# A gated MLP on one core: the order of the first products, the evictions and the casts

## The chip, the core and the metric

The kernel runs on one core of a Trainium2 chip. A core has TensorE (PE in the profile, with its weight loads shown apart as PEld), VectorE (DVE), ScalarE (ACT), GpSimd (POOL) and SyncE (SP, which here only issues transfers). They run side by side and meet at semaphores. Matrix products go to PSUM, eight banks of 512 fp32 values on each of 128 partitions; DVE and ACT take them out to SBUF. The metric is the device time of one execution in microseconds; lower is better.

## The reference

```python
def reference(x, w1, w2):            # x: 16 x 256 x 512, w1: 512 x 4096, w2: 2048 x 512, all fp32
    h = x @ w1
    gate, value = np.split(h, 2, axis=-1)
    h = np.maximum(gate, 0) * value
    return (h @ w2).astype(np.float32)
```

The 16 x 256 rows are 4096 tokens. The first layer makes 2048 gate and 2048 value columns for each, their gated product g is the input of the second layer.

## The kernel before

**Tiles and stages.** The tokens go through in four sets of 1024 (`s` from 0 to 3), each in two halves of 512 (`TH`). A set has a first layer of 16 blocks `jb` (128 hidden columns each, gate and value) and a second layer. Both layers are computed with seven products P1 to P7 in place of eight, on sums of the operands: `x_S1` to `x_S4` are sums of quarters of x (`x_sum`, line 451, on DVE), T1 to T4 are sums of quarters of the weights (`w1_one`, line 160, written to `wt` by POOL in set 0), and `g_S1` to `g_S4` are the sums of quarters of g (`g_sum`, line 275, on POOL and DVE) for the second layer. Operands are fp16, sums in PSUM fp32.

**Hybrid blocks.** Class `Block` holds the seven products, each of two 128x512 matmuls through `mm` (line 202). P1 goes to a bank X, ACT copies it to a bank Y (line 209); P2 adds to X, so it must come after that copy; P5 and P3 go to a bank W, P6, P7 and P4 add to Y. ACT and DVE combine the banks into g (lines 216 to 242). `SLOT` and `PERIOD` put the products of neighbouring blocks in a fixed interleaved order.

**Plain blocks.** In set 0 the weight sums are not there at the start, so the first four blocks (`NPLAIN`) are computed in the plain way, class `Plain`: `mm(side, a, q, n)` runs four matmuls (line 259) over the contraction for the gate (side 0, bank X) or the value (side 1, bank W), for quarter `q` of 256 tokens, or for both with `n = 2`. `close(h)` has ACT scale the value out of W (line 264) and DVE make g from it and X (line 265).

**The opening.** SP loads the first 512 tokens of x in fp32 (`xf`) and the first weight chunk (`wl`, gate half and value half), two transfers each, alternating (lines 406 and 407). POOL's queue loads everything else of the weights, and the second 512 tokens as fp16 (`xh`). `turn_pair(xo, b0)` transposes two 128-token blocks of x on PE into two W banks; DVE takes out the even block and ACT the odd one, into `x_A1` (line 377). `cast_w(g_)` casts one half of the first weight chunk to fp16: two of the four contraction quarters by ACT (line 391), two by DVE (line 392). `turn_half` does the transposes of the second 512 tokens, through an X bank (line 384 takes them out). `idle` issues matmuls with no use, to occupy PE while it waits for data.

**Buffers.** X has three PSUM banks, Y three, W two; transposes share the W and X banks with the products. All five engines' orders are written out by hand: each engine executes its instructions in the order in which the program emits them, and waits in front of one hold up those behind it.

**Set 0 beside the opening.** POOL makes the weight sums of blocks 4 to 15 in order, with the loads of w2 between (lines 523 to 539): T1 to T4 of blocks 12 to 15 come last, as four operations of 128x1024. They are followed by the sums of w2's quarters, made by accumulating transfers (`add_w2`, line 163), the fp16 copy of the next x (`cast_x`, line 359), and then `g_S1` and `g_S3` for rows 0 to 3 and `g_S1` for rows 4 and 5. At the end of set 0's first layer DVE makes `g_S1` for rows 6 and 7, then `g_S2`, `g_S4` and the second half of `g_S3` (lines 571 to 575). The second layer (`mm2_stream`, line 286) starts with products that need no sums (X), then P5 needs `g_S1`, P6 needs `g_S2`, P3 `g_S4`, P7 `g_S3`. Most of a set's second layer runs before the next set's first layer begins, the rest inside it.

Of the kernel before, what the change touches and what calls it, by code (L numbers as in the profile page):

```python
# [18 lines left out]
PERIOD = 7  # L19
NWARM = 8  # L20
NFILL = 2
NPLAIN = 4
HIGH, LOW = 512.0, 32.0
GS = 2.0 ** -19
SLOT = {"P1": 0, "P5": 1, "P2": 3, "P6": 4, "P3": 5, "P7": 9, "P4": 13}
# [74 lines left out]
def fast_way(ctx, tc, x2, w1, w2, out2, flag):  # L100
# [54 lines left out]
    def w1_ops(eng, jb, n):  # L155
        for t in TURNS:
            w1_one(eng, jb, n, *t)

    def w1_one(eng, jb, n, m, a, b, o):
        eng.tensor_tensor(W(m, jb, n), W(a, jb, n), W(b, jb, n), op=o)  # L160

    def add_w2(m, v):
        nc.gpsimd.dma_start(out=V[m], in_=V[v], accum_op=ADD)
# [7 lines left out]
    def idle(n):  # L171
        for _ in range(n):
            t = psy.tile([P, TH], F32, name="Y", tag="Y")
            nc.tensor.matmul(t, warm_b[:, :P], warm_b[:, :TH], start=True, stop=True)

    def x_tiles():
        o = {f"A{h}": xpool.tile([P, 4, TH], F16, name=f"x_A{h}") for h in (1, 2)}
        for h in (1, 2):
            for k in (1, 2):
                o[f"A{h}{k}"] = o[f"A{h}"][:, 2 * k - 2:2 * k]  # L180
        for n in ("S1", "S2", "S3", "S4"):
            o[n] = xpool.tile([P, 2, TH], F16, name=f"x_{n}")
        return o
# [88 lines left out]
    def g_sum(eng, go, n, h0, h1):  # L272
        for m, i0, i1, op in SUMS:
            if m == n:
                eng.tensor_tensor(go[n][:, h0:h1], go[i0][:, h0:h1], go[i1][:, h0:h1], op=op)  # L275
# [69 lines left out]
    def advance(stream, n):  # L345
        for _ in range(n):
            if stream is None or next(stream, 0) == 0:
                return
# [5 lines left out]
    def fetch_w2(i):  # L354
        ks, n = slice(i // 2 * NHC, i // 2 * NHC + NHC), i % 2
        nc.gpsimd.dma_start(out=w2_h[n][:, ks], in_=w2_v[:, ks, n * HALF:(n + 1) * HALF])

    def cast_x(s):
        nc.gpsimd.dma_start(out=x16[s], in_=x2[s * SET:(s + 1) * SET, :])

    def g_tiles():
        g = gpool.tile([P, NJ, SET], F16, name="g")
        gs = {n: gpool.tile([P, NHC, TH], F16, name=f"g_{n}") for n in ("S1", "S2", "S3", "S4")}
        return g, g_ops(g, gs)

    g, go = g_tiles()
# [4 lines left out]
    def turn_pair(o, b0):  # L371
        for b in (b0, b0 + 1):
            ps = psw.tile([P, 4, P], F32, name="W", tag="W")
            for e in range(4):
                nc.tensor.transpose(ps[:, e], xf[:, b, e * P:(e + 1) * P], ident[F32])
            copy = nc.scalar.copy if b % 2 else nc.vector.tensor_copy
            copy(out=o["A1"][:, :, b * P:(b + 1) * P], in_=ps)  # L377
# [8 lines left out]
    def turn_by_dma(s, o, h):  # L386
        for k in range(2):
            nc.sync.dma_start_transpose(out=o[f"A{h + 1}{k + 1}"], in_=x16[s][h * TH:(h + 1) * TH, k * 256:k * 256 + 256])

    def cast_w(g_):  # L390
        nc.scalar.copy(out=wr[0][:, :2, g_], in_=wl[:, :2, g_])
        nc.vector.tensor_copy(out=wr[0][:, 2:, g_], in_=wl[:, 2:, g_])
# [3 lines left out]
    def fetch_rows(s, q):  # L396
        rows[s, q] = xpool.tile([P, 2, D], F16, name=f"xn{q % 2}")
        nc.sync.dma_start(out=rows[s, q], in_=x16[s][q * 256:(q + 1) * 256].rearrange("(b p) d -> p b d", p=P))

    def look_x(s, i):  # L400
        b = i // 2
        t = rows[s, b // 2][:, b % 2] if s else (xf, xh)[b // NB][:, b % NB]
        look(t[:, i % 2 * 256:i % 2 * 256 + 256], 4 * NB * s + i, 256)
# [14 lines left out]

    xo = x_tiles()
    plain = [Plain(g, jb) for jb in range(NPLAIN)]  # L420
    idle(NWARM)
    cast_w(0)
    turn_pair(xo, 0)
# [2 lines left out]
    plain[1].open_x()  # L426
    for p in plain[:2]:
        p.mm(0, xo["A1"], 0)
    cast_w(1)
    turn_pair(xo, 2)  # L430
    for p in plain[:2]:
        p.open_w()
        p.mm(1, xo["A1"], 0)
    for p in plain[:2]:
        p.mm(0, xo["A1"], 1)
        p.mm(1, xo["A1"], 1)
        p.close(0)
    for p in plain[2:]:
        p.open_x()
# [9 lines left out]
    def x_sum(o):  # L449
        n, i0, i1, op = sums.pop(0)  # L450
        nc.vector.tensor_tensor(o[n], o[i0], o[i1], op=op)

    for p in plain:
        p.open_x()
        p.open_w()
        if p is plain[0]:
            for q in range(2):
                p.mm(0, xo["A2"], q)
                p.mm(1, xo["A2"], q)
        else:  # L460
            p.mm(0, xo["A2"], 0, 2)
            p.mm(1, xo["A2"], 0, 2)
        x_sum(xo)
        if p is not plain[-1]:
            p.close(1)
        look_x(0, p.jb)
# [47 lines left out]
    for s in range(NS):  # L514
        if s:
            g, go = g_tiles()
        first = NPLAIN if s == 0 else 0
        blocks = {jb: Block(xo, g, jb) for jb in range(first, NJ)}
        plan = {jb * PERIOD + at: (jb, n) for jb in blocks for n, at in SLOT.items()}
        last = NJ * PERIOD  # L520
        stream = mm2_stream(s, go)
        if s == 0:
            w1_ops(nc.gpsimd, 4, 2)
            fetch_w2(0)
            fetch_w2(1)
            w1_ops(nc.gpsimd, 6, 2)
            fetch_w2(2)
            fetch_w2(3)
            w1_ops(nc.gpsimd, 8, 2)
            w1_ops(nc.gpsimd, 10, 2)  # L530
            for to, v in ((V["T1"], V["B11"]), (v_12, w2_h[1]), (V["T4"], V["B21"])):
                nc.sync.dma_start(out=to, in_=v)
            for t in TURNS:
                w1_one(nc.gpsimd, 12, 4, *t)
                if t[0] == "T2":
                    add_w2("T1", "B12")
                    add_w2("T3", "B22")
            add_w2("T2", "T1")
            cast_x(1)
        for at in range(first * PERIOD, last + PERIOD):  # L540
            if at in plan:
                jb, n = plan[at]
                if n == "P1" and s and jb in (4, 8):
                    fetch_rows(s, 1 + jb // 4)
                if n == "P2" and s == 0 and jb in (11, 13, 15):
                    h = jb - 11
                    if h == 4:
                        add_w2("T4", "T2")
                    for m in ("S1", "S3")[:2 - h // 4]:
                        g_sum(nc.gpsimd, go, m, h, h + 2)  # L550
                getattr(blocks[jb], n)()
                ended = jb - (n == "P7") if n == "P7" or (n, jb) == ("P4", NJ - 1) else -1
                if ended in blocks:
                    blocks[ended].finish()
                if n == "P5":
                    for f in LOOKS.get((s, jb), ()):
                        f()
                if ended >= 0 and s:
                    if ended < NHC:
                        g_sum(nc.gpsimd, go, "S3", ended, ended + 1)  # L560
                        if s == 1 and ended in (1, 4):
                            cast_x(2 + ended // 4)
                    elif ended < NJ - BY_DVE:
                        for m in ("S1", "S2", "S4"):
                            g_sum(nc.gpsimd, go, m, ended - NHC, ended - NHC + 1)
            elif at >= last:
                advance(stream, 4)
            else:
                advance(prev, 4)
        if s == 0:  # L570
            g_sum(nc.vector, go, "S1", 6, 8)
            for m in ("S2", "S4"):
                for h in (0, NHC // 2):
                    g_sum(nc.vector, go, m, h, h + NHC // 2)
            g_sum(nc.vector, go, "S3", NHC // 2, NHC)
        else:
            for m in ("S1", "S2", "S4"):
                g_sum(nc.vector, go, m, NHC - BY_DVE, NHC)
        done = 20
        if s + 1 < NS:  # L580
            xo = x_tiles()
            for h in range(2):
                turn_by_dma(s + 1, xo, h)
            for q in range(2):
                fetch_rows(s + 1, q)
            advance(stream, 100)
            sums = list(SUMS)
            for _ in SUMS:
                x_sum(xo)
            if s == 0:  # L590
                w1_ops(nc.vector, 0, 2)
                w1_ops(nc.vector, 2, 2)
            advance(stream, MM2 - TAIL - 100 - done)
        else:
            advance(stream, MM2)
        prev = stream
# [29 lines left out]
```

## Time and profile before

| | |
|---|---|
| median of 5 runs | 311.81 us (311.71 to 312.69) |
| the profiled execution, its own time | 311.87 us |
| its span, first to last instruction | 310.1 us |
| TensorE's mean granted clock | 0.999 |
| DMA: bytes, mean rate | 30.74 MB, 99 GB/s |

By stage (a table of the busy time of each engine, in us):

| stage, us | PE | DVE | ACT | POOL |
|---|---|---|---|---|
| 0 to 10 | 7.22 | 2.10 | 3.19 | 6.76 |
| 10 to 26 | 15.23 | 9.59 | 7.85 | 11.77 |
| 26 to 63 | 37.00 | 31.75 | 24.89 | 34.17 |
| 63 to 73 | 9.37 | 9.36 | 6.72 | 3.27 |
| 73 to 302 | 229.00 | 163.04 | 145.50 | 92.03 |
| 302 to 310.1 | 3.54 | 1.27 | 0.77 | 0.00 |

In the rows of the profile, "engine line op out<-in" names an instruction by the source line that emits it and by its tiles; X, Y and W are the PSUM banks above. A bracket `[1.1 <-DVE ...]` after a row is the idle time of the engine just before it and what ended it. A chain of waits lists, in order of time, the work on which the end of a stretch depended.

### The profile page before, as it was taken

What the parts mean: (1) busy time and instruction counts of PE and PEld (TensorE: products, weight loads), DVE (VectorE), ACT (ScalarE), POOL (GpSimd) and SP (SyncE); (2) the same over time, 40 slices, a digit from 0 to 9 for tenths busy, and PEclk for the clock granted to TensorE, in tenths of its full rate; (3) what the DMA queues carried; (4) which work ended last, traced back from release to release, by engine and by line L of the source; (5) the groups of instructions that cost most, each with busy time, mean ns of one, the idle gap of its engine ahead of it and who ended that gap; (6) DMA issues with size and microseconds to landing.
All of it is one profiled execution on the core that took longest, in us unless ns stands there. A gap on an engine that the chain in (4) does not pass through costs nothing.

```text
span 310.1 us, 5097 instructions
## 1 busy us (share of the span) xinstructions
PE 301.4 (97%) x1867; PEld 182.6 (59%) x1867; DVE 217.1 (70%) x330; ACT 188.9 (61%) x450; POOL 148.0 (48%) x135
## 2 busy tenths in 40 slices
PE   7899999999999999999999999999999999999994
PEld 4654444588854444478874444458884444447883
DVE  1377888898548888884338888886526888888401
ACT  3347767547667666648847666656857666673230
POOL 5679997950003537992001435995000434899000
PEclk9999999999999999999999999999999999999999
DMA  7999979979223480045220110028311101000113
GB/s 254 189 202 204 217 195 234 203 119 235 113 78 85 88 169 0 3 87 156 98 104 35 34 34 2 0 50 153 140 71 68 34 2 34 0 2 0 66 71 140
DMA packets 33449, 30.74 MB, mean 99 GB/s; under 512 B 13872, under 2 KB 27952, under 8 KB 33200
## 3 DMA queue, kind: packets, MB, share of 16 engines
q0 software_dynamic: 10704, 11.54, 23.1%
q1 hardware_dynamic: 22576, 18.75, 20.6%
q8 instruction: 15, 0.25, 0.3%
q10 hardware_dynamic: 144, 0.13, 0.1%
q14 instruction: 10, 0.08, 0.1%
HBM read 24.12 MB, written 11.53 MB: 115 GB/s over the span
## 4 chain that ended last, share of the span: by engine, by line
PE 92%; DMA 2%; DVE 2%; issue 1%; ACT 1%; SPq 0%; DVEq 0%
PE Y L202 25%; PE X L202 17%; PE W L202 17%; PE Y L286 13%; PE W L286 8%; PE X L286 8%; DMA g<-in_w_dram 2%; PE W L259 2%; PE X L259 2%; DVE g_S L275 1%; ACT x_A L384 0%; SPq L406 0%; DVE g L241 0%; DVE x_A L377 0%; ACT Y L209 0%
## 5 line engine op out<-in xcount | busy, mean ns | idle before, releaser
L275 POOL TENSOR_TENSOR g_S<-g 128x512 f16<-128x512 f16 (+1 forms) x47 | 60.6, 1331 | 125.3 <-DVE g L241 123.4
L202 PEld LDWEIGHTS <-wt 128*128 128x128 f16 x480 | 46.9, 98 | 55.0 <-issue 0.2
L202 PE MATMUL X<-x_A,wr 128*128 128x512 f16 x240 | 71.4, 379 | 0.2 <-ACT Y L209 0.2
L202 PE MATMUL Y<-x_S,wt 128*128 128x512 f16 x240 | 71.4, 379 | 0.0
L202 PEld LDWEIGHTS <-wr 128*128 128x128 f16 x360 | 35.2, 98 | 41.0 <-issue 0.5
L229 DVE SCALAR_TENSOR_TENSOR cc<-W,pu 128x512 f32<-128x512 f32 x60 | 41.5, 692 | 23.8 <-ACT pu L223 23.7
L209 ACT COPY Y<-X 128x512 f32<-128x512 f32 x60 | 34.2, 570 | 37.7 <-PE X L202 37.1
L286 PEld LDWEIGHTS <-g_S 128*128 128x128 f16 x512 | 49.9, 98 | 6.9 <-DVE g_S L275 1.2
L235 DVE SCALAR_TENSOR_TENSOR cc<-Y,pu 128x512 f32<-128x512 f32 x60 | 41.5, 691 | 6.2 <-PE Y L202 0.2
L223 ACT ACTIVATE pu<-Y 128x512 f32<-128x512 f32 x60 | 35.8, 597 | 14.3 <-PE Y L202 14.3
L230 DVE SCALAR_TENSOR_TENSOR g<-X,cc 128x512 f16<-128x512 f32 x60 | 41.5, 692 | 2.3
L286 PEld LDWEIGHTS <-g 128*128 128x128 f16 x384 | 37.6, 98 | 8.2
L241 DVE SCALAR_TENSOR_TENSOR g<-Y,cc 128x512 f16<-128x512 f32 x60 | 40.9, 682 | 1.8 <-PE Y L202 1.8
L216 ACT ACTIVATE pu<-W 128x512 f32<-128x512 f32 x60 | 36.1, 602 | 0.0
L202 PE MATMUL W<-x_S,wt 128*128 128x512 f16 x120 | 35.7, 379 | 0.0
L202 PE MATMUL W<-x_S,wr 128*128 128x512 f16 x120 | 35.7, 379 | 0.0
L202 PE MATMUL Y<-x_A,wt 128*128 128x512 f16 x120 | 35.7, 379 | 0.0
L286 PE MATMUL X<-w,g 128*128 128x256 f16 x256 | 31.2, 273 | 0.0
L286 PE MATMUL Y<-v,g_S 128*128 128x256 f16 x256 | 30.7, 273 | 0.3 <-DVE g_S L275 0.3
L316 DVE SCALAR_TENSOR_TENSOR o<-W,pv 128x256 f32<-128x256 f32 x16 | 6.8, 424 | 30.3 <-PE W L286 30.3
L275 POOL TENSOR_TENSOR g_S<-g,g_S 128x512 f16<-128x512 f16 x18 | 21.8, 1210 | 1.4
L275 POOL TENSOR_TENSOR g_S<-g_S,g 128x512 f16<-128x512 f16 x18 | 21.3, 1186 | 1.4
(69 smaller groups left out, 297.0 us busy)
## 6 DMA issues: line engine op xcount, KB each, us to landing
out_dram<-o SPq DMA_DIRECT2D x16, 256.0 KB, 2.2
out_dram<-pv SPq DMA_DIRECT2D x15, 256.0 KB, 2.0
x<-in_x_dram POOLq DMA_DIRECT2D x3, 1024.0 KB, 9.3
xn<-x SPq DMA_DIRECT2D x12, 256.0 KB, 3.4
wr<-in_w_dram POOLq DMA_DIRECT2D x4, 512.0 KB, 14.2
w<-in_w_dram POOLq DMA_DIRECT2D x4, 512.0 KB, 11.7
wr<-in_w_dram POOLq DMA_DIRECT2D x6, 256.0 KB, 9.0
g_S<-in_x_dram SPq DMA_DIRECT2D x2, 512.0 KB, 4.7
```

The lines of the kernel that those rows point to most:

```text
L202: nc.tensor.matmul(ps, W(wn, self.jb)[:, b], self.xo[xn][:, b, :], start=fresh and b == 0, stop=b == 1, skip_group_check=True)
L209: nc.scalar.copy(out=self.Y, in_=self.X)
L216: nc.scalar.activation(self.p5, self.W, COPY, scale=GS)
L223: nc.scalar.activation(self.u2, self.Y, COPY, scale=-GS)
L229: nc.vector.scalar_tensor_tensor(out=self.c12, in0=self.W, scalar=GS, in1=self.u2, op0=MULT, op1=ADD)
L230: nc.vector.scalar_tensor_tensor(out=self.g[:, self.jb, :TH], in0=self.X, scalar=0.0, in1=self.c12, op0=MAX, op1=MULT)
L235: nc.vector.scalar_tensor_tensor(out=self.c22, in0=self.Y, scalar=-GS, in1=self.p5, op0=MULT, op1=ADD)
L241: nc.vector.scalar_tensor_tensor(out=self.g[:, self.jb, TH:], in0=self.Y, scalar=0.0, in1=self.c22, op0=MAX, op1=MULT)
L259: nc.tensor.matmul(ps[:, ts], W(name, self.jb)[:, e % 2], a[:, e, ts], start=e == 0, stop=e == 3, skip_group_check=True)
L275: eng.tensor_tensor(go[n][:, h0:h1], go[i0][:, h0:h1], go[i1][:, h0:h1], op=op)
L286: nc.tensor.matmul(ps, go[gn][:, k, b * P:(b + 1) * P], V[vn][:, k, :], start=fresh and k == 0, stop=k == NHC - 1, skip_group_check=True)
L316: nc.vector.scalar_tensor_tensor(out=d["o1"][:, HALF:], in0=d["W"], scalar=1 / GS, in1=d["pu"][:, 1], op0=MULT, op1=ADD)
```

## The change

In the opening, the second gate quarters of the first two plain blocks are issued ahead of their value products, and the value products run over all 512 tokens at once (four matmuls of 512 columns in place of twice four of 256, for each block). The transposes of x blocks 2 and 3, with their evictions on DVE and ACT, are emitted ahead of the cast of the value weights. W banks are opened after both gate quarters. The first hybrid block (block 4) is made ahead of the plain loop, and its P1, with ACT's copy from X to Y, is emitted inside the last plain block's second half, between its gate products and its value products; P1 is taken out of the later plan for that block.

```diff
     xo = x_tiles()
     plain = [Plain(g, jb) for jb in range(NPLAIN)]
+    lead = Block(xo, g, NPLAIN)
     idle(NWARM)
     cast_w(0)
     turn_pair(xo, 0)
...
     for p in plain[:2]:
         p.mm(0, xo["A1"], 0)
+    turn_pair(xo, 2)
     cast_w(1)
-    turn_pair(xo, 2)
+    for p in plain[:2]:
+        p.mm(0, xo["A1"], 1)
     for p in plain[:2]:
         p.open_w()
-        p.mm(1, xo["A1"], 0)
-    for p in plain[:2]:
-        p.mm(0, xo["A1"], 1)
-        p.mm(1, xo["A1"], 1)
+        p.mm(1, xo["A1"], 0, 2)
         p.close(0)
...
             p.mm(0, xo["A2"], 0, 2)
+            if p is plain[-1]:
+                lead.P1()
             p.mm(1, xo["A2"], 0, 2)
...
         blocks = {jb: Block(xo, g, jb) for jb in range(first, NJ)}
-        plan = {jb * PERIOD + at: (jb, n) for jb in blocks for n, at in SLOT.items()}
+        if s == 0:
+            blocks[first] = lead
+        plan = {jb * PERIOD + at: (jb, n) for jb in blocks for n, at in SLOT.items() if (s, jb, n) != (0, first, "P1")}
```

## The prediction

> **What bounds the kernel now.** I read the page's busy times first, then TensorE's own waits over the whole span, then the chain of waits in two stretches (the first 26 us and 60 to 73 us), and last the timeline of POOL and DVE from 48 to 72 us.
>
> ```profile
> PE 301.4 (97%) x1867; PEld 182.6 (59%) x1867; DVE 217.1 (70%) x330; ACT 188.9 (61%) x450; POOL 148.0 (48%) x135
> ```
>
> ```profile
> PE W L259 <- DVE x_A L377: 1.1, 1, 1.1
> PE X L259 <- ACT x_A L377: 0.6, 1, 0.6
> PE W L286 <- DVE g_S L275: 0.3, 1, 0.3
> PE Y L286 <- DVE g_S L275: 0.3, 1, 0.3
> PE X L259 <- ACT x_A L384: 0.3, 1, 0.3
> PE X L202 <- ACT Y L209: 0.2, 1, 0.2
> ```
>
> TensorE is the bound, and these few waits (total, times, longest), with 1.3 us before its first matmul, are all that the view has for it: four before 26 us, in the stretch that the change reorders, and two on g_S, at 69.16 and 71.43 us. From 73 to 302 us a table by stage has PE busy 229.00 of 229.00 us, so whatever shift remains after 71.43 us reaches the end, and nothing else does.
>
> The waits of the opening, in the chain of the first 45 us (start, length, what):
>
> ```profile
> 9.62 0.61 DVE x_A L377
> 10.28 1.03 PE W L259 x8
> ...
> 25.23 0.58 ACT Y L209
> 25.85 0.59 PE X L202 x2
> ```
>
> The last weight half of the first chunk lands at 9.17; DVE and ACT cast it, only then turn out x blocks 2 and 3, and PE resumes at 10.28. At 25.85 P2 may add to X only after ACT has copied X to Y.
>
> Now the stage where a shift must pass: POOL's, DVE's and PE's part of the timeline (start, duration, engine, line).
>
> ```profile
> 48.40 0.88 POOL L163 DMA_DIRECT2D v<-w  x1 [2.51 <-DMA v<-w]
> 48.99 2.46 POOL L160 TENSOR_TENSOR wt<-wr 128x1024 f16<-128x1024 f16 x1
> 51.07 2.45 POOL L160 TENSOR_TENSOR wt<-wr,wt 128x1024 f16<-128x1024 f16 x1
> ...
> 62.63 1.49 POOL L163 DMA_DIRECT2D v_T<-v  x1
> 63.25 3.02 POOL L275 TENSOR_TENSOR g_S<-g 128x1024 f16<-128x1024 f16 x1
> ```
>
> ```profile
> 63.67 0.69 DVE L241 SCALAR_TENSOR_TENSOR g<-Y,cc 128x512 f16<-128x512 f32 x1 [0.45 <-PE Y L202]
> 64.40 2.43 DVE L275 TENSOR_TENSOR g_S<-g 128x1024 f16<-128x1024 f16 x1
> 66.75 2.35 DVE L275 TENSOR_TENSOR g_S<-g_S,g 128x2048 f16<-128x2048 f16 x2
> ```
>
> ```profile
> 69.16 1.48 PE L286 MATMUL Y<-v,g_S 128*128 128x256 f16 x12 [0.28 <-DVE g_S L275]
> ...
> 71.43 1.48 PE L286 MATMUL W<-w,g_S 128*128 128x256 f16 x12 [0.35 <-DVE g_S L275]
> ```
>
> From 48.40 POOL runs without a gap until 66.27, and it started there on a DMA landing, not on TensorE. PE at 69.16 and 71.43 waits for DVE's S2 and S4, whose first step (64.40, S1 of rows 6 and 7) took 2.43 us beside POOL's S1 of rows 4 and 5.
>
> [...] DVE's 128x1024 sum takes 0.69 us at 138.20, where it came just ahead of POOL (POOL's 1.16 us sum then took 1.69), and 1.53 at 138.92, [...] at 24.30 an x sum took 0.98 beside POOL's DMA issues, [...] the granted clock was 1.00 from 5 to 12 us with a 1.1 us wait inside, so the shorter waits below should not touch it.
>
> **The change part by part.** Matmul pace from the chain: 256 columns 0.1085 us (eight gate matmuls, 7.23 to 8.10), 512 columns 0.216 (pairs 0.431 apart).
>
> First plain blocks. DMAs and POOL's queue keep their order. x blocks 2 and 3 land at 7.8 and are turned from 8.10 to about 9.15, as before. Their evictions now stand ahead of the casts on both engines: DVE 8.7 to 9.4, ACT 9.2 to 9.8 (0.68 and 0.58 in the rows). They wait for the transposes, and behind them stand only the casts, whose data lands at 9.17. The casts end at 9.83 (DVE, 0.43) and 10.40 (ACT, 0.62). PE starts the second gate quarters at 9.8; eight take 0.87, to 10.7, and cover the ACT cast. The value products follow, eight of 512 columns where there were sixteen of 256: 8 x 0.216 = 1.73, to 12.4. Before, this point came at 12.89. Gain 0.47 (0.5).
>
> What is late next: the second chunk's gate half is there at 11.06 and needed at 12.4, its value half 12.39 against 13.3, the second half of x 13.66 and 14.94 against about 13.9 and 16.3. The closest has some 0.2 us; so no new wait, or one below 0.2. The 0.3 us wait for the second turned half (18.54) moves along, since its ACT copy hangs on the same products.
>
> P1 amid the last plain block. No instruction is added: the first hybrid block's two P1 matmuls go ahead of four value matmuls. The X to Y copy (0.57 and 0.2 for the matmul's end) now has four value and two P5 matmuls over it, 6 x 0.216 = 1.30. The bubble before P2, 25.85 less 25.45 (P1 at 24.59 and two pairs), goes: 0.40. X has three buffers; P1's was freed by the DVE step at 22.08 + 0.68 = 22.76, earlier now by 0.5, against a need at 23.2. ACT's order changes by one place: the copy stands ahead of one 0.41 us square, which no matmul waits for.
>
> Sum in PE's clock at 26 us: 0.47 + 0.40 = 0.87, bounds 0.7 to 1.0.
>
> First toll: the last weight sums. P4 of block 12 needs T4 of blocks 12 to 15, which POOL ends at 51.07 + 2.45 = 53.52. PE's P4 stood at 53.95. It cannot start before about 53.58 (0.05 for the signal, as between ACT's cast end 9.82 and PE's load 9.86). So 0.37 is left, and 0.5 turns into a new wait of PE on POOL, in part (0.1 or so) one P7 earlier, on T3 at 51.45 against 52.22. POOL's times do not move with PE: its start at 48.40 hangs on a copy of w2 that SP sends at 43.31, when the last w2 load has landed (43.23), and the queue of these loads is never empty from 8 to 43 us.
>
> Second toll[...]. Block 15's last gate product ends at 64.36 - 0.37 = 63.99[...]. POOL, done with its DMA issue at 62.63 + 1.49 = 64.12, then wants 2.15 us for its own S1. If POOL is first, all is as before: POOL to 66.27, DVE S1 to 66.83. If DVE is first, [...] POOL follows to 66.8, and DVE's S2 waits for that end. Either way S2 starts at about 66.8[...]. The gain left is that one start, 64.12 less 64.03: 0 to 0.1, taken as 0.06. S2, S4 (four halves, 1.14 apart) and PE at 71.43 follow.
>
> After that nothing moves. The DMA transposes at 63.91 wait for the fp16 x, landed at 63.83, also.[...]
>
> Total: 311.87 - 0.06 = 311.81 for the profiled execution, which lies 0.06 above the median of the runs; so 311.75 against 311.81.
>
> **Rivals.** (a) A part is carried: [...] Then 0.37 arrives: 311.44. For it: PE's waits at 69.16 and 71.43 hang on DVE alone. Against: the 2.43 us of S1. (b) All is carried, because POOL's run from 48.40 comes earlier too: its start is a DMA landing, and the runs of before spread from 311.71 to 312.69, so landings may vary. 0.87 less gives 310.94. Against: nothing in the edit brings a landing forward. (c) Slower: the x sums come 0.5 earlier on DVE[...], where POOL makes the weight sums and then issues the w2 loads (23.11 and 29.69). Two of the four sums delayed POOL by about 0.55 each before; two more would cost 1.1, and if POOL's run at 48.40 slips by that, the end does: 312.91. It decides only once the queue of DMAs runs dry: the first w2 load was issued by 24.04, the load ahead of it landed at 31.29, so several microseconds of slack stand against it. A late landing for another reason has the same price. (d) The change does not do what it says: P1's buffer or the evictions hold PE as before. The order of issue and the waits named above speak against it, and the time would be the same 311.8.
>
> **How the numbers follow.** Forecast and (d), no shift past 71.43 us: 0.56. (a) 0.12, (b) 0.18, (c) 0.14. What a measurement of this kernel tells from no change is about 0.2%, 0.62 us; (a) lies inside it. So faster 0.19 (b and a sliver of a), same 0.66, slower 0.15. The range runs from 311.0, which takes in (a) and the edge of (b), to 312.3, half of (c).
>
> **What would show it.** PE's wait for ACT's Y copy and most of its 1.1 us on DVE's x_A gone; the first L202 pair after the last plain block some 0.9 earlier; a new wait of PE's weight load on POOL's L160 near 53.5; DVE's S1 at about 64.0, or POOL's S1 ending near 66.8; PE's last wait on g_S still near 71.4. I am wrong if PE passes 53.5 without that wait, if S2 on DVE starts clearly before 66.7, or if POOL's start at 48.40 has moved.

## The result and the profile after

| us | before | after |
|---|---|---|
| median | 311.86 (47 runs) | 313.23 (26 runs) |
| lowest to highest | 311.12 to 313.79 | 311.49 to 313.87 |
| profiled execution, own time | 311.87 | 313.54 |
| its span | 310.1 | 311.8 |

The ratio is 1.0035, with an interval of 1.0025 to 1.0045: the change costs 0.35%, where no change was forecast. Of the 26 runs after, four lie at 311.5 to 311.8, as before; the others lie between 312.4 and 313.9.

First the busy times of the kernel after (time, share of the span, instructions).

```profile
PE 301.9 (97%) x1859; PEld 181.5 (58%) x1859; DVE 217.7 (70%) x330; ACT 188.8 (61%) x450; POOL 147.4 (47%) x135
```

The work is the same, and PE has eight matmuls and eight weight loads fewer than before (1859 against 1867): where sixteen value matmuls of 256 columns stood, there are eight of 512. These 16 instructions turn out to matter.

PE's waits in the kernel after (total, times, longest):

```profile
PE X L259 <- ACT x_A L377: 1.5, 2, 0.8
PE Y L174 <- DVE warm L167: 1.3, 1, 1.3
PE Y L202 <- POOL wt L160: 1.1, 2, 0.9
PE Y L286 <- DVE g_S L275: 0.5, 1, 0.5
PE W L286 <- DVE g_S L275: 0.3, 1, 0.3
PE X L259 <- ACT x_A L384: 0.3, 1, 0.3
```

The wait for ACT's copy Y is gone, as is DVE's x_A at the head of the list; on ACT's x_A PE waits 1.5 us in two parts, where it was 0.6 in one. New is a wait of 1.1 us on POOL's weight sums, in two parts. Where PE stands at the start, from its timeline after (start, duration, engine, line):

```profile
10.07 1.03 PE L259 MATMUL X<-x_A,wr 128*128 128x256 f16 x8 [0.67 <-ACT x_A L377]
10.94 1.89 PE L259 MATMUL W<-x_A,wr 128*128 128x512 f16 x8
12.66 0.59 PE L259 MATMUL X<-x_A,wr 128*128 128x512 f16 x2
...
25.23 0.59 PE L202 MATMUL X<-x_A,wr 128*128 128x512 f16 x2
```

The second gate quarters (10.07) come ahead of the merged value products (10.94); the next plain block starts at 12.66 where it stood at 12.89, and P2 of block 4 at 25.23 where it stood at 25.85. So PE is 0.62 us ahead at 25 us. By 73 us it is 1.52 us behind, and what turned it round is on POOL (the part of its timeline after in which it was gapless before):

```profile
49.96 0.88 POOL L163 DMA_DIRECT2D v<-w  x1 [4.32 <-DMA v<-w]
50.54 2.43 POOL L160 TENSOR_TENSOR wt<-wr 128x1024 f16<-128x1024 f16 x1
52.63 2.41 POOL L160 TENSOR_TENSOR wt<-wr,wt 128x1024 f16<-128x1024 f16 x1
...
64.81 2.98 POOL L275 TENSOR_TENSOR g_S<-g 128x1024 f16<-128x1024 f16 x1
```

The run of POOL that began at 48.40 begins at 49.96, after an idle 4.32 us (2.51 before) on the landing of a transfer `v<-w`: SP's copy of 1 MB of w2 from one place in SBUF to another, to which POOL adds another quarter. Not all of these additions follow the weight sums of blocks 12 to 15: this one and one more stand between their T2 and their T3, so T3 and T4 wait behind the landing (T3 starts at 50.54, 48.99 before). SP sent the copy at 43.07, a little sooner than before (43.31), but it took 6.31 us instead of 4.52. From there on every step is late by the same amount, on DVE, and on PE (its timeline after follows DVE's):

```profile
65.56 2.79 DVE L275 TENSOR_TENSOR g_S<-g 128x1024 f16<-128x1024 f16 x1
68.27 2.35 DVE L275 TENSOR_TENSOR g_S<-g_S,g 128x2048 f16<-128x2048 f16 x2
```

```profile
53.03 0.60 PE L202 MATMUL Y<-x_S,wt 128*128 128x512 f16 x2 [0.93 <-POOL wt L160]
...
72.95 1.27 PE L286 MATMUL W<-w,g_S 128*128 128x256 f16 x10 [0.35 <-DVE g_S L275]
```

| us | before | after | later by |
|---|---|---|---|
| copy of w2 sent | 43.31 | 43.07 | -0.24 |
| copy of w2 landed | 47.83 | 49.38 | 1.55 |
| POOL's run starts | 48.40 | 49.96 | 1.56 |
| T4 of the last blocks ends | 53.52 | 55.05 | 1.53 |
| POOL's `g_S1` for rows 4, 5 ends | 66.27 | 67.79 | 1.52 |
| DVE's `g_S2` starts | 66.75 | 68.27 | 1.52 |
| PE's last wait on `g_S` ends | 71.43 | 72.95 | 1.52 |
| last matmul starts | 305.27 | 306.79 | 1.52 |

From that wait to the last matmul it is 233.84 us in both. The rest of the 1.7 us of span is the tail, 4.97 instead of 4.82.

Why did the copy take longer? The transfers by queue, packets, MB and share of 16 engines: first of the kernel before from 42 to 43 us, then of the kernel after from 46.5 to 47.6 us.

```profile
q0 software_dynamic: 25, 0.01, 8.9%
q8 instruction: 1, 0.02, 6.5%
```

```profile
q1 hardware_dynamic: 93, 0.37, 89.6%
q8 instruction: 1, 0.02, 5.2%
```

The kind "instruction" is one packet of 16 KB, one of 15 in an execution, by its name a piece of an engine's program. PE executed 1867 matmuls and 1867 weight loads before, some 249 for each of the 15 packets, and no other engine over 450 instructions that the profile counts, so I take the packets as PE's. Before it ran at 42.49 for 1.04 us, to 43.53. The copy, sent at 43.31, moved nothing yet: the busy share of the DMA engines from 43 to 48 us, in 40 slices of 0.125 us, begins in the kernel before with eleven empty slices, to 44.37.

```profile
DMA  0000000000099099689499599995994956999899
```

After, the packet ran at 46.59 for 0.92 us, in the midst of the copy (SP's queue, q1). And from 48.7 to 49.4 us, where the copy's last packet ends and the next copy of SP's queue goes on, the kernel after shows this:

```profile
q0 software_dynamic: 31, 0.13, 96.2%
q1 hardware_dynamic: 5, 0.02, 5.8%
```

One engine of 16 is 6.3%. All that SP's queue moved there, 5 packets and 5.8%, is no more than one engine's time, while POOL's next transfer took 96.2%. From these shares I infer that the copies on SP's queue hung on a single engine's last packets, one after another.

The records of single packets and signals in the trace show the lag directly. The landing of the copy is counted by 16 signals. Before, they came from 47.28 to 47.83. After, 15 of them had come by 47.65, sooner than the last one before; the sixteenth came at 49.38. The fetch began as one 8 KB packet of the copy ended, and the packet that began as the fetch ended took 0.81 us, where the median of the copy's 128 packets is 0.33. Two more packets, within 1.6 us ahead of the fetch, took 0.62 and 0.60; before, none took over 0.46. The records do not name the DMA engine. If all these fell on one, the fetch's 0.92 and what the three packets took above the median come to about 2.0 us (an estimate), which is enough for the 1.8 of the copy.

So the theory: **the edit shortens PE's program by 16 instructions, which moves the fetch of PE's next 16 KB into the copy of w2, and the copy's landing sets POOL's run.** The rivals: the moved work itself (new order, P1) delays POOL or the copy in some other way; the copy's length varies from execution to execution and has nothing to do with the edit.

### The profile page after: what moved, and what is told of

Read it like the earlier page. It is cut to its first block, busy times and chain, and to the rows that moved or that the text cites. A ratio compares the mean times of both kernels' runs of the same rounds, so it can differ in the third digit from the quotient of the medians.

```text
span 311.8 us, 5081 instructions
## 1 busy us (share of the span) xinstructions
PE 301.9 (97%) x1859; PEld 181.5 (58%) x1859; DVE 217.7 (70%) x330; ACT 188.8 (61%) x450; POOL 147.4 (47%) x135
## 4 chain that ended last, share of the span: by engine, by line
PE 78%; DMA 10%; POOL 6%; issue 2%; DVE 1%; ACT 0%; SPq 0%; DVEq 0%; POOLq 0%
PE Y L202 21%; PE X L202 14%; PE W L202 14%; PE Y L286 13%; PE W L286 8%; PE X L286 8%; DMA w<-in_w_dram 4%; POOL wt L160 4%; DMA wr<-in_w_dram 3%; DMA v<-w 2%; DVE g_S L275 1%; DMA g_S<-in_x_dram 1%; POOL w L356 1%; POOL wr L352 1%; POOL g_S L414 0%
```

## The experiments

Times are medians, each beside the kernel before on the same chip, as ratio with interval. "Fetch" is the start of the 16 KB packet near 43 us, "copy" the time of w2's copy from send to landing, "POOL" the start of the addition behind it.

| kernel | PE's instructions, against before | fetch | copy | POOL | median | ratio |
|---|---|---|---|---|---|---|
| before | 0 | 42.49 | 4.52 | 48.40 | 311.86 | 1 |
| after | -16 | 46.59 | 6.31 | 49.96 | 313.23 | 1.0035 [1.0025, 1.0045] |
| after again | -16 | 46.75 | 6.34 | 50.12 | 313.32 | 1.0031 [1.0020, 1.0043] |
| after, 16 put back (e1) | 0 | 42.72 | 4.57 | 48.10 | 311.71 | 0.9991 [0.9979, 1.0004] |
| the same, other form (e5) | 0 | 42.51 | 4.46 | 47.92 | 311.95 | 0.9992 [0.9983, 1.0001] |
| after, 8 put back (e6) | -8 | 43.01 | 5.20 | 48.75 | 312.07 | 0.9996 [0.9984, 1.0008] |
| after, 32 put in (e7) | +16 | 41.14 | 4.51 | 47.96 | 311.58 | 0.9989 [0.9979, 0.9999] |
| gate order and merge alone (e2) | -16 | 48.46 | 4.46 | 48.14 | 311.97 | 1.0010 [0.9996, 1.0025] |
| P1 alone (e3) | 0 | 42.93 | 4.50 | 48.38 | 312.00 | 0.9995 [0.9982, 1.0009] |

**The instructions put back.** To the kernel after, matmuls of 32 columns are added in the opening, where PE waits for data anyway: eight of them with their weight loads make 16 instructions. In e1 they begin a new sum in a Y bank, and a part of the kernel's result is changed by it; which sums were not traced.

```diff
+    def small(n):
+        t = psy.tile([P, TH], F32, name="Y", tag="Y")
+        for _ in range(n):
+            nc.tensor.matmul(t[:, :32], warm_b[:, :P], warm_b[:, :32], start=True, stop=True)
...
     idle(NFILL)
+    small(4)
...
     turn_pair(xo, 2)
+    small(4)
```

> The changed kernel with 16 PE instructions more: eight matmuls of 32 columns without use (each with its weight load), four where PE waits for the first evictions and four where it waits for the second, so that PE's program is as long as before and PE's time is not. Theory F (a 16 KB instruction fetch, which in the changed kernel falls at 46.59 us, into the copy of w2 from 43.07, and holds one DMA engine for 0.92 us): the fetch goes back to about 42 us, the copy takes about 4.5 us instead of 6.3, POOL's chain starts near 48.2, time 311.3 to 311.8. Theory G (PE being ahead by 0.7 us, or the order of the evictions, sets off the slow copy): nothing changes, 313.2. Theory N (chance of the chip on that day): 311.9, as before.

e5 adds the same number in a form that leaves every sum as it was: the short matmuls add to the bank of an idle matmul.

```diff
+        return t
+
+    def small(t, n):
+        for _ in range(n):
+            nc.tensor.matmul(t[:, :32], warm_b[:, :P], warm_b[:, :32], start=False, stop=True, skip_group_check=True)
...
-    idle(NFILL)
+    small(idle(NFILL), 4)
...
     turn_pair(xo, 2)
+    small(idle(1), 3)
```

> The 16 PE instructions once more, in a form that keeps every product of the kernel: four short matmuls behind the matmuls without use that are there already, one more of these and three short ones where PE waits for the second evictions. Theory F (the instruction fetch): fetch near 42.7 us, copy of w2 about 4.5 us, 311.5 to 311.9, ratio to before 0.999 to 1.000. Theory N (the first form was a lucky hour): 313.

Both bring the fetch back to where it was and with it the copy, and the time: 0.9991 and 0.9992, with intervals that both take in 1. POOL's restart and DVE's first sum in e5, from the two timelines:

```profile
47.92 0.88 POOL L163 DMA_DIRECT2D v<-w  x1 [2.29 <-DMA v<-w]
```

```profile
64.35 1.98 DVE L280 TENSOR_TENSOR g_S<-g 128x1024 f16<-128x1024 f16 x1
```

All that the edit reorders is still in these kernels, so the reordering isn't what costs, and the first rival falls; adding work to PE made the kernel faster, by 0.43% between the ratios of after and e5, some 1.3 us. e6 puts back only the first four matmuls, e7 puts in twice as many as e5.

```diff
     turn_pair(xo, 0)
-    idle(NFILL)
+    small(idle(NFILL), 4)        # e6; in e7 8
...
     turn_pair(xo, 2)
+    small(idle(1), 7)            # e7 alone
```

> The changed kernel with 8 PE instructions more, half the dose (four short matmuls at the first wait). Theory F: the fetch comes some 0.9 us earlier than in the changed kernel, at 44 to 46 us, still inside the copy that starts at 43.1, so 312.5 to 313.4, slower than before. A theory in which any added instruction cures it: 311.7.

> The changed kernel with 32 PE instructions more, twice the dose. Theory F: the fetch comes before the copy starts, at 41 to 42.7 us, so 311.5 to 311.9, no better than 16. If it is the exact length of the program that counts (a landing place, not a time), it could be slow again.

In e6 the packet starts at 43.01 and takes 1.28 us, to 44.29, so it overlaps only the head of the copy, whose packets move from 44.1 on; the copy takes 5.20, between the two other lengths: a fetch at the head of the copy went with 0.7 us more of it and not 1.8. The time of 312.5 or more that was expected did not come. The median is 312.07, and neither from before nor from e5 can the intervals tell it. In e7 the fetch comes 1.35 us earlier than in before, and the time is as expected; its ratio is the lowest of these four, but the four intervals overlap.

**The same kernel again.** The kernel after once more, unchanged, beside its own runs of the kernel before.

> The changed kernel once more, beside the others of this call on one chip. Theory F: the fetch inside the copy in most executions, 312.9 to 313.5; theory N (that day's chip): 312.0.

The fetch is at 46.75, the copy takes 6.34 us, and the ratio is 1.0031. The long copy is no accident of one execution, and the second rival falls. That the times after do spread, with four of 26 like before, fits a fetch that sometimes falls beside the copy, but no trace of such an execution was taken.

**One part alone.** e2 takes the kernel before and makes only the new order of the gate quarters and the merged value products.

```diff
     for p in plain[:2]:
-        p.open_w()
-        p.mm(1, xo["A1"], 0)
-    for p in plain[:2]:
         p.mm(0, xo["A1"], 1)
-        p.mm(1, xo["A1"], 1)
+    for p in plain[:2]:
+        p.open_w()
+        p.mm(1, xo["A1"], 0, 2)
         p.close(0)
```

> The kernel before with one part of the change: the second gate quarters ahead of the value products and the value products over 512 columns (16 PE instructions fewer), the evictions behind the casts as before, P1 where it was. Theory F: the fetch falls into the copy as in the changed kernel, about 313.2. Theory G: no early eviction and no gain for PE, so 311.9. By the prediction's sum PE gains next to nothing here, under 0.1 us.

The expectation missed: 311.97, though PE has the 16 instructions less. In the profiled execution the fetch ran at 48.46, behind the copy, which took 4.46 us. The delay then fell on the next copy (`v_T`, landed at 50.64 instead of 49.15), which had room. So it isn't the number of instructions by itself that costs, but where the fetch falls; four of the 22 runs of e2 took 313.49 to 314.24, the others 312.75 at most. e3 makes only the other part, P1 amid the last plain block, with the number of instructions kept:

```diff
+    lead = Block(xo, g, NPLAIN)
...
             p.mm(0, xo["A2"], 0, 2)
+            if p is plain[-1]:
+                lead.P1()
             p.mm(1, xo["A2"], 0, 2)
```

> The kernel before with the other part alone: P1 of block 4 inside the last plain block. PE's program is as long as before; PE gains the bubble of 0.40 us. Theory F: the fetch stays near 42 us, the copy stays at 4.5 us[...]: 311.7 to 311.9. Theory G: a part of the slowing, 312.3 or more.

It gives 0.9995, no change, with POOL at 48.38. The bubble before P2 is gone: from the third plain block to P2 it is 12.57 us (13.38 to 25.95), as after. But the weights landed later in the profiled execution (9.66, against 9.17), so PE has no lead at P6 (26.38, against 26.28 before) and does not wait for the weight sums. That the 0.4 us would end there and at DVE's and POOL's sums, as forecast, this trace does not show. It shows the same end as before: `g_S2` on DVE starts at 66.73 and PE's last wait on `g_S` ends at 71.40.

**POOL freed of the copy.** If the copy's landing costs only because POOL stands waiting for it in front of the weight sums, then moving the addition `add_w2("T3", "B22")` behind them takes the fetch's price away. One edit, made on the kernel after (e4), on before (e11 and e15, the same kernel twice) and on after with e5's 16 instructions (e8 and e14, the same kernel twice).

```diff
                 w1_one(nc.gpsimd, 12, 4, *t)
                 if t[0] == "T2":
                     add_w2("T1", "B12")
-                    add_w2("T3", "B22")
+            add_w2("T3", "B22")
             add_w2("T2", "T1")
```

> The changed kernel with POOL's two last weight sums of blocks 12 to 15 (2.1 us each) put ahead of the accumulating transfer that waits for the copy of w2, so that POOL works while the copy runs. Both theories say that POOL's chain from the copy on sets the end, so both expect a gain here: POOL's weight sums end at about 50 instead of 55, PE does not wait for them, its g_S work starts at about 54.5 and the end comes at 311.0 to 311.4 even with a slow copy, 310.8 with a fast one. If the chain is not what sets the end, 313.2 stays.

> The changed kernel with both cures: POOL's last weight sums ahead of the transfer that waits for the copy, and 16 PE instructions more so that the fetch does not fall into the copy. If both theories of the chain hold, POOL goes from its weight sums to the transfer without a wait, its g_S work starts near 53.6, and the time is 311.1 to 311.5, at or a little below the reordering alone (311.56), with less spread. If the fetch alone was the loss, it equals the 311.7 of the padded kernel.

> The kernel before with POOL's two last weight sums of blocks 12 to 15 ahead of the transfer that waits for the copy, nothing else. It frees the chain that held back the changed kernel. With it PE's lead should count: the version with both cures and the change took 311.10, and without the change PE is behind by its 0.4 to 0.6 us of opening, so 311.4 to 311.8 if the opening counts once POOL is out of the way, 311.1 if the change is worth nothing even then.

> The changed kernel with both cures (POOL's order and 16 PE instructions) again, on one chip with the next: 311.1. If the change is worth its opening once POOL is out of the way, it is 0.3 to 0.6 us below the next.

> The kernel before with POOL's order alone, again, beside the version with both cures: 311.4 to 311.7 if the change is worth something once the chain is freed, 311.1 if it is worth nothing.

| kernel | copy | POOL's weight sums end | median | ratio |
|---|---|---|---|---|
| after, POOL's order (e4) | 5.29 | 49.85 | 311.56 | 0.9985 [0.9974, 0.9996] |
| before, POOL's order (e11) | 4.87 | 50.19 | 311.44 | 0.9978 [0.9968, 0.9988] |
| the same (e15) | 5.43 | 50.15 | 311.49 | 0.9985 [0.9976, 0.9993] |
| after, order and 16 (e8) | 4.70 | 50.05 | 311.10 | 0.9963 [0.9949, 0.9977] |
| the same (e14) | 4.41 | 49.88 | 310.83 | 0.9961 [0.9948, 0.9975] |

In POOL's timeline of e4 the addition no longer waits, because it comes 0.83 us after the copy's landing (sent at 43.37, 5.29 us later landed):

```profile
47.43 2.42 POOL L160 TENSOR_TENSOR wt<-wr,wt 128x1024 f16<-128x1024 f16 x1
49.49 1.21 POOL L163 DMA_DIRECT2D v<-w  x1
52.51 0.85 POOL L163 DMA_DIRECT2D v<-v_T  x1 [1.81 <-DMA v_T<-w]
```

But e4 missed its 311.0 to 311.4, and it is no faster than e11 and e15, which lack the change. The last row suggests why: POOL, freed of one landing, waits 1.81 us for the next one, 0.63 in e14. Its `g_S` work starts at 53.60, where it starts at 52.45 in e14, and PE still waits 0.24 us on `g_S`, to 70.44.

e8 and e14 are faster than before and after. What PE still waits for in e14 after its first matmul, all of it before 19 us, and DVE's first sum there:

```profile
PE X L264 <- DVE x_A L382: 0.9, 1, 0.9
PE X L264 <- ACT x_A L382: 0.4, 1, 0.4
PE X L264 <- ACT x_A L389: 0.3, 1, 0.3
```

```profile
64.38 0.69 DVE L280 TENSOR_TENSOR g_S<-g 128x1024 f16<-128x1024 f16 x1
```

Neither a wait on POOL nor one on `g_S` is left, and DVE's sum takes 0.69 us, where beside POOL's it took 2.79 in the kernel after. Now the gain of the opening can reach the end, and e14 against e15, on one chip, shows it: P6 starts at 25.93 against 26.63, and the product that follows on `g_S4` at 70.44 against 70.81. The medians are 0.66 us apart, the two profiled executions 0.77 (310.79 and 311.56); 0.37 of it is located there, and the rest of this pair lies in the tail behind the last matmul, so of the 0.66 only the 0.37 is shown to come from the edit. That the lead at P6 is no accident of this pair, all the traces with the whole change show: P6 starts in them at 25.44 to 26.04, and at 26.20 to 26.77 in those with PE's order of before.

**A fetch imitated.** Three kernels add a 16 KB transfer of ACT's queue to the kernel before, emitted after P5 of block 10: e9 copies a row of w1 into a scratch row in DRAM, e12 one partition of g into such a row, e13 two rows of 8 KB into one partition of `g_S3` and of `g_S4` before these are computed.

```diff
+    junk = dpool.tile([1, J], F32, name="junk")            # e9; in e12 [1, 8 * SET], F16
...
                 getattr(blocks[jb], n)()
+                if (s, jb, n) == (0, 10, "P5"):
+                    nc.scalar.dma_start(out=junk, in_=w1[:1, :])                                      # e9
+                    nc.scalar.dma_start(out=junk, in_=g[:1, :8].rearrange("p a t -> p (a t)"))        # e12
+                    nc.scalar.dma_start(out=row, in_=w1[:1, i * 2048:(i + 1) * 2048])                 # e13, i = 0, 1; row: in g_S3, g_S4
```

> The kernel before, its PE program untouched, with one 16 KB transfer more (a row of w1 to a DRAM scratch row that nobody reads), issued by ACT at about 44.0 us so that its packet falls into the copy of w2 as the instruction fetch does in the changed kernel. Theory F: one DMA engine lags, the copy takes 5.3 to 6.3 us instead of 4.5, POOL's chain from 48.4 slips by 0.8 to 1.8 us and the time is 312.6 to 313.6. If a packet of this size in the copy is not the cause: 312.0 as before (ACT's 0.4 us for the issue hangs on nothing).

> The kernel before, its PE program untouched, with one 16 KB transfer more out of a single partition (a finished row of g to a DRAM scratch row that nobody reads), issued by ACT at about 43.4 us. In the earlier form the 16 KB were spread as 16 packets of 1 KB[...] (46.04 to 47.36) and the copy of w2 was hardly delayed. If the packets now stay on one DMA engine, theory F (one engine occupied for about 0.9 us lags, and all wait for it) expects the copy at 5.3 to 6.3 us, POOL's chain later by 0.8 to 1.8 us, 312.8 to 313.6. If they are spread again, 312.0 to 312.4. If one engine is occupied and the time stays 312.0, theory F is wrong in its mechanism.

> The kernel before, its PE program untouched, with two transfers of 8 KB from DRAM, each into one partition of a buffer that is idle then (g_S3 and g_S4, overwritten later), issued by ACT at about 43.8 and 44.3 us. Both should stay on one DMA engine and[...] hold it near 46 us. Theory F: that engine's part of the copy of w2 lags, POOL's accumulating transfer starts at 49.2 to 50.0 instead of 48.4, and the time rises by as much: 312.7 to 313.5. If the copy keeps its 4.5 us, what slows it in the changed kernel is more than the time of a packet.

| kernel | added packets | copy | POOL | median | ratio |
|---|---|---|---|---|---|
| e9 | 16 of 1 KB, 46 ns each | 5.45 | 48.39 | 312.38 | 1.0009 [0.9999, 1.0019] |
| e12 | one of 16 KB at 45.50, 0.645 us | 4.76 | 48.66 | 312.76 | 1.0026 [1.0010, 1.0043] |
| e13 | two of 8 KB at 47.13 and 48.07, 0.31 us | 5.02 | 48.46 | 312.54 | 1.0015 [1.0006, 1.0023] |

These tell little of the 1.8 us. In e9 the transfer was spread over many packets, so it wasn't the thing to be imitated; its copy was sent 0.94 us earlier (42.37) and landed at 47.82, as before. What lengthened it there may as well be the fetch, which ran from 42.52 to 43.85, over the copy's first packet at 43.49. In e13 the two packets came at the copy's end and behind it. Only in e12 did a whole 16 KB in one packet fall into the midst of the copy: 15 of the copy's signals had come by 47.79, the last at 48.08. In that execution POOL started 0.26 us later than before, and the last wait on `g_S` ended 0.24 later (71.67). The copy's other packets were not slowed, none took over 0.47 us, which is a difference from the fetch. The further time of e12 lies behind the last matmul: the tail is 5.57 us, against 4.82 before.

**All traces together.** The dose can be read off all 17. In nine of them the fetch was over when the copy's first packet moved, or came behind its last; the copy took 4.41 to 4.76 us. In six the fetch overlapped the copy's head (e4, e6, e9, e11, e13, e15); it took 4.87 to 5.45. In the two with the fetch in its midst, both of the kernel after, it took 6.31 and 6.34.

**What stays open.** Why packets of the copy near a fetch take 0.6 to 0.8 us; why the fetch ran 4.1 us later than before, where 16 instructions, eight matmuls of 0.216 us, are 1.7 us; and what the added transfers do to the tail. On the second the traces give a hint, no more. In e4, with the PE program of after, the fetch ran at 44.27, 1.78 later than before, and just ahead of the copy's first packet (44.50). In after, e10 and e2 the copy's first packet came at 44.19 to 44.34, and the fetch 2.4 to 4.2 us behind it. A fetch that comes a little too late and then waits behind the copy's packets would fit; that it waits there is a guess, which no record shows. That the packet belongs to PE's program is inferred: from the number of PE's instructions, and because only that number was varied in e1 and e5 to e7, and the packet moved.

## Why the prediction was wrong

**The opening.** Mis-sized. The order came as described, but x blocks 2 and 3 landed at 8.17 instead of 7.83 and the value weights at 9.54 instead of 9.17 in this execution, so the second gate quarters began at 10.07 instead of 9.8. The gain at the next plain block was 0.23 and not 0.47.

**P1.** Right. From that block to P2 it is 12.57 us (25.23 less 12.66), 12.96 before: 0.39 gained where 0.40 was forecast, and no wait for ACT's copy is left.

**The first toll.** This is the step that failed, and in it one sentence: that POOL's times do not move with PE, since its start at 48.40 hangs on a copy that SP sends at 43.31. The dependence was read rightly, the wait on T3 and T4 came, and nothing in the edit moves the copy's sending. But its length was taken as given, at 4.52 us; it took 6.31. The halved number of value matmuls was priced in PE's time alone, and not as a shorter program whose fetches fall elsewhere. The landing came 1.55 us later, and POOL's start moved to 49.96, which the prediction had named as a sign of being wrong. So the toll was not the gain but more: PE waits 0.93 us at T3 and 0.17 at T4.

The trace has the packets of this kind on a queue of their own (q8), 16 KB each, with some 249 counted PE instructions for each packet, and PE's list of waits has none on a fetch. What it shows is a cost to another transfer: the fetch ran for 0.92 us amid the copy, whose 8 KB packets show one that ended as it began (46.59) and one that began as it ended (47.49). That alone doesn't give the 1.8 us.

**The second toll.** Held, as far as it was put to the test. DVE's 128x1024 sum took 2.43 us before, 2.79 after and 1.98 in e5 beside POOL's, and 0.69 in e14. That the two sums would run one after the other, whichever came first, was the prediction's estimate, from such durations; why they are slow beside each other was not shown. DVE's first sum ended 0.56 us after POOL's before and after (66.27 and 66.83; 67.79 and 68.35), though DVE came at 64.40 in one and 65.56 in the other; and 0.56 after it in e5 (65.77 and 66.33). If POOL's sum begins where its DMA issue ends, as the prediction took it, DVE came 0.28 us behind POOL before (64.40 and 64.12) and 0.08 ahead of it after (65.56 and 65.64), and ended last both times, so on that reckoning being first did not help it. In e5 it came 0.74 behind POOL (64.35 and 63.61), so the 0.09 of the forecast was not tested there. In e14 POOL's `g_S` work began 1.83 us sooner than before (52.45, 54.28); if it took the same 11.99 us (to 66.27), it ended at 64.44 (an estimate), about when DVE came, at 64.38. That all past 71.43 us passes one for one to the end holds too.

**The rivals.** (a) and (b) fell: the gain was carried only where POOL's order was changed and the fetch kept out of the copy (e8, e14), and not with the order alone (e4). (d) fell, the change does what it says. (c), slower at 312.91, had the right place and nearly the right price, and named a late landing for another reason in its last sentence; its mechanism, x sums that delay POOL, isn't what happened. Of POOL's four weight sums from 17.78 on, two took 1.48 and 1.60 us beside x sums, before as after, and the other two 1.15 to 1.16; so nothing was added there, and each had been longer by 0.32 to 0.45, not by 0.55. POOL's weight sums ahead of the copy's landing ran 0.26 us sooner (T2 at 42.62, before at 42.88), and the copy was sent sooner, not later. With the fetch out of the way the forecast of no change holds, in e1 and e5 within 0.1% of before.

## What to carry to other kernels

An edit that changes the number of an engine's instructions can move its later instruction fetches: here 16 of PE's instructions less moved one from 42.49 to 46.59 us. A fetch is a packet among the other transfers (16 KB, 0.88 to 1.47 us here): where a transfer's landing sets the pace with no slack, look for the packets of the kind "instruction" beside it, in the old trace and in the new. When an edit that only takes work away makes a kernel slower, put the same number of short instructions back before blaming the order. The more lasting cure is slack: let the engine do other work before it waits for the landing. Here that alone took 0.15 to 0.22% off the kernel before (e11, e15); the gain made upstream came through only with the fetch out of the copy as well (e8, e14).

## What was not expected of the hardware

- A 16 KB instruction packet took 0.88 to 1.47 us in the traces of before and after; in the midst of a 1 MB copy it went with 1.8 us more for that copy, at its head with 0.35 to 0.93, and ahead of it with 0.2 at most.
- The copy's packet that began as the fetch ended took 0.81 us in both traces of the kernel after, where the median is 0.33.
- One 16 KB transfer out of a single partition was one packet too, 0.645 us long (e12); 16 KB from a row in DRAM became 16 packets of 1 KB, 46 ns each (e9).
- The tail behind the last matmul's start isn't fixed: 4.73 to 5.14 us in the 14 traces without an added transfer, 5.20 to 5.57 in the three with one.
